# A one-core decoder trunk whose turned blocks land as whole block rows, and whose next reader puts them in order

## The chip, the cores and the metric

The kernel runs on one core of a Trainium2 chip. The metric is the device time of one execution in microseconds. TensorE (PE in the rows) multiplies, VectorE (DVE) and ScalarE (ACT) work elementwise, GpSimd (POOL) does a few powers and transfers, SyncE (SP) issues nearly all transfers. Each engine works through its own list in order, and semaphores tie the lists together.

## The reference

One layer over 256 positions of width 2048. A normalised input is projected by one wide matrix; three branches of width 1024 read slices of the result: a gated linear recurrence (A), a sparse attention with compressed, selected and window keys (B), and a softmax attention with a cumulative forget bias (C). Each branch output is gated, projected to 2048, weighed and summed; two more 2048 x 2048 products follow.

```python
z = split_columns(rms_norm(h, ln_gain) @ w_in + b_in)
y_a = rglru_branch(z['lru_x'], ...) * silu(z['lru_gate'])
q_b = rms_norm(split_heads(z['nsa_q'], 8), nsa_q_gain)
k_s = rms_norm(split_heads(z['nsa_k_slc'], 2), nsa_k_gain)   # k_w and k_c alike
y_b = nsa_branch(q_b, k_c, v_c, k_s, v_s, k_w, v_w, g_b) * silu(z['nsa_gate'])
y_c = fox_branch(rms_norm(fox_q, fox_q_gain), rms_norm(fox_k, fox_k_gain), fox_v, log_f) * silu(z['fox_gate'])
merged = sum(sigmoid(merge)[i] * (y_i @ w_branch[i]) for i in range(3))
h = h + merged @ w_out
h = h + sigmoid(h @ w_ple_gate) * rms_norm(p @ w_ple, ple_gain)
```

A gain of a query and a gain of its keys multiply the same channel of one dot product.

## The kernel before

**Weights.** All weights stream once from memory as 384 blocks of 128 x up to 1024 numbers (`raw`, five buffers, L399). ScalarE rounds each block to a short format (`wh`) and VectorE takes the rest (`wl`, L416): one *cut*. Each product is three matmuls, `wh` by the high half, `wl` by the high half, `wh` by the low half of the other factor (L382). The three blocks at the start are cut in smaller pieces, so that the cut with number n on ScalarE, counted from 0, belongs to block n - 4. A block of 1024 columns of the wide projection is 12 matmuls of 512 columns; a compression block ("cmp", every fourth or so from block 26 on) is 8 short ones. There are four pairs of `wh` and `wl` (L413), so cut n can start only when TensorE has left block n - 8. The transfer of block n into `raw` is issued when cut n - 5 is done.

**Side work.** Between blocks run generators (norms, LRU steps, attention tasks). A planner with a clock of its own (`Clock`, `Side`, L156 to L320) takes steps from them while VectorE and ScalarE are less than `LIMITS` behind TensorE; it writes the order of every engine. Everything is recorded through one helper, so the profile puts all on L206 and rows are told apart by the names of tiles.

**Turning.** A block with positions on partitions is turned to channels on partitions by `cross` (L654): VectorE transposes 32 x 32 cells into `zt`, and four transfers on SyncE's queue, one for each group of 32 partitions, put the cells in their place, each cell row of 32 numbers (128 bytes) at its own address (L667). `landed` then lets the planner wait `LAND`, 7000 ns of its clock. The gate and `lru_x` chunks are turned by `turn_chunk` (L673) and read by `silu_cols` and `biased_cols`; queries and keys by `norm_rows` (L842); the softmaxes inside `nsa_task` (L879) and `fox_task` (L990); the merged rows and h by `split_turned` (L1069). There are 41 such groups of four transfers.

**Factors.** Queries are scaled by their gain over sqrt(128) (`gqn`, `gqf`), keys by theirs (`vcol("nk")`, `vcol("fk")`), each in the split.

**LRU.** `lru_task` (L710) has four instances; each puts a table load, eight sigmoids, two tanh, a table load, two exponentials, a square and a root on ScalarE.

Of the kernel before, what the change touches and what calls it, by code (L numbers as in the profile page):

```python
# [323 lines left out]
def block_kernel(ctx: ExitStack, tc: tile.TileContext, io):  # L324
# [265 lines left out]
    def vec_task():  # L590
        a = VEC["lru_gate"]
        V.tensor_scalar(vec[:, a:], vec[:, a:], 0.5, None, op0=OP.mult)
        nl = sml([P, 8], name="nl")
        V.tensor_scalar(nl, vec[:, VEC["lam"]:VEC["lam"] + 8], -1.0, None, op0=OP.mult)
        yield from softplus(spc, nl, 8)
        V.tensor_scalar(spn, spc, -8.0, None, op0=OP.mult)
        V.tensor_scalar(spc, spc, 8.0, None, op0=OP.mult)
        V.tensor_scalar(gqn, vcol("nq"), SCALE, None, op0=OP.mult)
        V.tensor_scalar(gqf, vcol("fq"), SCALE, None, op0=OP.mult)
        yield True  # L600
# [31 lines left out]
    def silu_cols(dst, k0, src, name):  # L632
        for c in range(2):
            hb = vcol(name, k0 + c)
            t = one([P, S], name="th")
            x = dst[:, k0 + c, :]
            A.activation(t, src[:, c * S:(c + 1) * S], AF.Tanh, bias=hb, scale=0.5)
            A.activation(x, src[:, c * S:(c + 1) * S], AF.Identity, bias=hb, scale=0.5)
            V.scalar_tensor_tensor(x, t, 1.0, x, op0=OP.add, op1=OP.mult)

    def biased_cols(dst, k0, src, name):
        for c in range(2):
            A.activation(dst[:, k0 + c, :], src[:, c * S:(c + 1) * S], AF.Identity, bias=vcol(name, k0 + c))

# [28 lines left out]
    def turn_chunk(read, out, into, dst, k0, name):  # L673

        yield from side.wait("rs")
        yield from side.room(k4=1)
        x = flat(dst[:, k0:k0 + 4, :])
        for t, z in enumerate(celled(x)):
            A.activation(z, cells(out[t]), AF.Copy, scale=rsr[:, t:t + 1])
        side.done.add(read)  # L680
        yield from cross(x, x)
        side.give(k4=1)
        yield from side.wait("vec")
        for q in range(0, 4, 2):
            into(dst, k0 + q, flat(dst[:, k0 + q:k0 + q + 2, :]), name)
            yield True

    def turn_cmp(read, out, into, dst, k0, name):

        yield from side.wait("rs")  # L690
        z = [two([P, 512], name="z") for _ in range(NT)]
        for t in range(NT):
            A.activation(z[t], out[t], AF.Copy, scale=rsr[:, t:t + 1])
            yield True
        side.done.add(read)
        yield from side.settle()
        yield from side.wait("vec")
        for q in range(2):
            b, = yield from side.take()
            for c in range(2):  # L700
                for t in range(NT):
                    T.transpose(banks[b][:, c * S + t * P:c * S + (t + 1) * P],
                                z[t][:, (2 * q + c) * P:(2 * q + c + 1) * P], ident)
            yield True
            into(dst, k0 + 2 * q, banks[b], name)
            side.back(b)
            yield True
# [89 lines left out]
    def cmp_end():  # L797
# [39 lines left out]
        yield from side.wait("kk")  # L837
        split(st["kh"][:, :, 256:256 + NCMP], st["kl"][:, :, 256:256 + NCMP], src, vcol("nk"))
        side.back(b)
        yield True  # L840

    def norm_rows(z, n, dst):  # L842
# [10 lines left out]
        yield from side.powers()  # L853
        yield from side.room(k4=1)
# [24 lines left out]
    def nsa_task(g, pr, t):  # L879
# [3 lines left out]
        n = t + 1  # L883
        yield from side.room(k1=3, k4=2)
        qh, ql = one([P, 2, P], R32, name="qh"), one([P, 2, P], R32, name="ql")
        split(qh, ql, qn[:, heads[0]:heads[0] + 2, t, :], gqn)
        yield from side.settle()
# [3 lines left out]

        p, pz = mid([P, 4, 4 * n, 32], name="prob"), mid([P, 4, 4 * n, 32], name="pz")
        ps = p.rearrange("p b n j -> p (b n j)").rearrange("p (a w k) -> p a w k", a=2, w=2)
# [41 lines left out]
        yield from cross(pt, pt, p)  # L935
        side.give(k4=1)
        yield from side.room(k4=2)
        pth, ptl = mid([P, 2 * n, 2, P], R32, name="pth"), mid([P, 2 * n, 2, P], R32, name="ptl")
        split(*(x.rearrange("p i a q -> p (i a q)") for x in (pth, ptl)), pt)
        side.give(k4=1)  # L940
        yield True
# [18 lines left out]
        T.matmul(out, vc3[:, g, :], pct.rearrange("p a q -> p (a q)"), start=False, stop=True)  # L960
        side.give(k1=2, k4=2)
        yield True
        A.activation(qn[:, heads[0]:heads[0] + 2, t, :], out.rearrange("p (a q) -> p a q", a=2), AF.Copy)
        side.back(b)
# [25 lines left out]
    def fox_task(h):  # L990
# [40 lines left out]
        pth, ptl = two([P, 3 * P], R32, name="fpth"), two([P, 3 * P], R32, name="fptl")  # L1031
        split(pth, ptl, pt)
        side.give(k2=1)
# [5 lines left out]
        yield True  # L1039
        A.activation(fq[:, h].rearrange("p t d -> p (t d)"), banks[b][:, :S], AF.Copy)  # L1040
        side.back(b)
        yield True


    def y_split(name, src, names, gate=None):
        yield from side.wait(*names)
# [4 lines left out]
        for i in range(0, 8, 2):  # L1051
            s = src[:, i:i + 2, :]
            if gate is not None:
                V.tensor_tensor(s, s, gate[:, i:i + 2, :], op=OP.mult)
            split(yh[:, i:i + 2, :], yl[:, i:i + 2, :], s)
            side.done.add(f"{name}{i // 2}")
            yield True

    def start(name):
        if name == "ysplit0":  # L1060
            side.urge(name, y_split(name, st["yl"], [f"lru{q}" for q in range(4)] + ["gl0", "gl1"], st["gl"]))
        elif name == "ysplit1":
# [5 lines left out]

    def split_turned(name, dst, j, x, src, scale=None):  # L1069

        hi, lo = dst[j // 2]
        yield from cross(flat(x), src)
        for k in range(0, 4, 2):
            to = slice(4 * (j % 2) + k, 4 * (j % 2) + k + 2)
            split(hi[:, to, :], lo[:, to, :], x[:, k:k + 2, :], scale)
            yield True


    def rows_task(h, out, bias):
# [27 lines left out]
        else:  # L1107
            key = "fq" if what == "fox_q" else "fk"
            if c == 0:
                st[key] = big([P, 8, NT, P], name=key)  # L1110
            side.urge(f"{key}{c}", norm_rows(z, 512, st[key][:, 4 * c:4 * c + 4].rearrange("p h t d -> p (h t d)")))

# [45 lines left out]
    def proj_chunk(h, out):  # L1158
# [12 lines left out]
        if b == 2:  # L1171
            if j == 0:
                st["mt"] = [(big([P, 8, S], R32, name="mth"), big([P, 8, S], R32, name="mtl")) for _ in range(2)]
            side.urge(f"mt{j}", split_turned(f"mt{j}", st["mt"], j, x, flat(x), 0.5))

    def out_chunk(h, out):
# [158 lines left out]

LAND = 7000.0
LIMITS = 4500.0, 4000.0
# [77 lines left out]
```

## Time and profile before

| what | value |
|---|---|
| time, median of 3 runs | 1074.43 us (1072.45 to 1078.02) |
| the profiled execution: its time, its span | 1075.37 us, 1073.6 us |
| TensorE busy | 1061.1 us, 99% of the span |
| VectorE, ScalarE busy | 770.2 us, 619.1 us |
| transfers of SyncE's queue | 192320 packets, 220.75 MB |
| packets under 512 bytes, all queues | 140984 of 197255 |

Busy time of TensorE is modelled and overlaps from matmul to matmul, so a row of busy time shows where it waited, and the distance between starts shows how much was lost.

### The profile page before, as it was taken

The numbers are of one execution on the slowest core, as the hardware profiler recorded it, in microseconds if no ns is written. First come the engines' busy times: TensorE is split into PE (matmuls) and PEld (weight loads), VectorE is DVE, ScalarE is ACT, GpSimd is POOL, SyncE is SP. The second block draws the span as 40 slices with busy tenths as digits, with TensorE's granted clock in tenths as the row PEclk, the third lists the DMA queues.
The fourth block names the chain that finished last, engine by engine and source line by source line (L and its number), as shares of the span: only waits on it lengthen the run. The fifth ranks groups of instructions, "written<-read, shape, count | busy, mean of one in ns | idle before, by whom it ended". The sixth has DMA issues, their size and how long they took to land.

```text
span 1073.6 us, 14079 instructions
## 1 busy us (share of the span) xinstructions
PE 1061.1 (99%) x4943; PEld 884.0 (82%) x4943; DVE 770.2 (72%) x1127; ACT 619.1 (58%) x905; POOL 51.9 (5%) x77
## 2 busy tenths in 40 slices
PE   9999999999999999999999999999999999999997
PEld 7888788788888888887888888888888888888886
DVE  7787689688678787878787776555766566666664
ACT  7568975895676556545654565465555444444442
POOL 0000001011000000011101000000000100000000
PEclk9999999999999999999999999999999999999999
DMA  9768677768777577577787676777677887788762
GB/s 339 220 207 255 209 202 216 278 219 236 210 228 203 162 212 228 144 219 231 226 241 215 207 235 176 226 211 212 198 220 240 257 254 213 232 244 260 278 209 78
DMA packets 197255, 237.54 MB, mean 221 GB/s; under 512 B 140984, under 2 KB 142144, under 8 KB 197184
## 3 DMA queue, kind: packets, MB, share of 16 engines
q1 hardware_dynamic: 192320, 220.75, 66.6%
q0 software_dynamic: 4720, 15.76, 5.6%
q8 instruction: 38, 0.62, 0.2%
q14 instruction: 33, 0.27, 0.1%
q10 hardware_dynamic: 144, 0.14, 0.0%
HBM read 215.62 MB, written 4.20 MB: 205 GB/s over the span
## 4 chain that ended last, share of the span: by engine, by line
PE 88%; ACT 4%; DVE 4%; issue 2%; DMA 1%; SPq 1%; ACTq 0%; DVEq 0%
PE main L206 84%; PE bank L206 4%; ACT wh L206 2%; DVE wl L206 2%; DMA raw<-in_w 1%; SPq L206 1%; ACT k_lru L206 1%; ACT L206 0%; ACT k_gl L206 0%; ACT k_th L206 0%; DVE k_uc L206 0%; DVE k_yl L206 0%; DVE k_qn L206 0%; DVE k_z L206 0%; DVE k_fq L206 0%
## 5 line engine op out<-in xcount | busy, mean ns | idle before, releaser
L206 DVE TENSOR_TENSOR wl<-raw,wh 128x1024 fp32r<-128x1024 f32 (+2 forms) x388 | 459.4, 1198 | 244.0 <-ACT wh L206 243.1
L206 ACT ACTIVATE wh<-raw 128x1024 fp32r<-128x1024 f32 (+2 forms) x388 | 398.8, 1039 | 319.9 <-PE main L206 258.5
L206 PE MATMUL main<-wl,k_hnh 128*128 128x512 f32 (+2 forms) x1026 | 394.9, 386 | 4.1 <-DVE wl L206 3.7
L206 PE MATMUL main<-wh,k_hnh 128*128 128x512 f32 (+2 forms) x1026 | 396.0, 387 | 2.2 <-ACT wh L206 2.1
L206 PE MATMUL main<-wh,k_hnl 128*128 128x512 f32 (+1 forms) x1024 | 393.4, 384 | 0.0
L206 PEld LDWEIGHTS main<-wl,k_hnh 128*128 128x128 f32 x1026 | 193.6, 189 | 43.3 <-DVE wl L206 7.1
L206 PEld LDWEIGHTS main<-wh,k_hnh 128*128 128x128 f32 x1026 | 193.4, 189 | 40.6 <-ACT wh L206 4.1
L206 PEld LDWEIGHTS main<-wh,k_hnl 128*128 128x128 f32 x1024 | 193.0, 189 | 37.9
L206 PE MATMUL main<-wh,k_yh 128*128 128x512 f32 x192 | 75.2, 392 | 0.0
L206 PE MATMUL main<-wh,k_yl 128*128 128x512 f32 x192 | 74.8, 389 | 0.0
L206 PE MATMUL main<-wl,k_yh 128*128 128x512 f32 x192 | 74.8, 389 | 0.0
L206 PE MATMUL main<-wh,k_mth 128*128 128x512 f32 x128 | 49.8, 389 | 0.0
L206 PE MATMUL main<-wl,k_mth 128*128 128x512 f32 x128 | 49.8, 389 | 0.0
L206 PE MATMUL main<-wh,k_mtl 128*128 128x512 f32 x128 | 49.8, 389 | 0.0
L206 PE MATMUL main<-wh,k_hth 128*128 128x512 f32 x128 | 49.8, 389 | 0.0
L206 PE MATMUL main<-wl,k_hth 128*128 128x512 f32 x128 | 49.8, 389 | 0.0
L206 PE MATMUL main<-wh,k_htl 128*128 128x512 f32 x128 | 49.8, 389 | 0.0
L206 PEld LDWEIGHTS main<-wh,k_yl 128*128 128x128 f32 x192 | 36.0, 188 | 7.6
L206 PEld LDWEIGHTS main<-wh,k_yh 128*128 128x128 f32 x192 | 36.1, 188 | 7.1
L206 PEld LDWEIGHTS main<-wl,k_yh 128*128 128x128 f32 x192 | 36.1, 188 | 7.0
L206 ACT ACTIVATE k_mg<-k_mg 128x512 f32<-128x512 f32 x24 | 15.2, 632 | 24.3 <-DVE k_mg L206 24.0
L206 PEld LDWEIGHTS main<-wh,k_mth 128*128 128x128 f32 x128 | 24.0, 188 | 5.0
(247 smaller groups left out, 965.8 us busy)
## 6 DMA issues: line engine op xcount, KB each, us to landing
raw<-in_w SPq DMA_DIRECT2D x369, 512.0 KB, 4.7
bias<-in_b_in POOLq DMA_DIRECT2D x21, 256.0 KB, 5.7
raw<-in_w SPq DMA_DIRECT2D x8, 408.0 KB, 4.4
k_pz<-k_prob SPq DMA_DIRECT2D x16, 128.0 KB, 4.1
e_dram<-k_e POOLq DMA_DIRECT2D x4, 512.0 KB, 3.6
k_merged<-k_zt SPq DMA_DIRECT2D x16, 128.0 KB, 3.3
k_xc<-in_x POOLq DMA_DIRECT2D x4, 512.0 KB, 5.4
k_hx<-k_zt SPq DMA_DIRECT2D x16, 128.0 KB, 3.3
```

What stands on the lines that cost most here:

```text
L206: r = call(out, *args, **kw)
```

## The change

`cross` no longer puts each 128-byte cell row in its place. Each of the four transfers writes to each partition its four whole block rows, of 1024 bytes at a full block, and the reader takes the cells in order by its access pattern (`moved`, `moved_heads`; `blocks` is the same view of a block already in order). `turn_chunk` now lands in a separate `zt` of 1024 columns. The gain of the keys is folded into `gqn` and `gqf`, the queries are split without a scale, and the key splits are made per 128 columns, since a moved view has one dimension more. The factor 0.5 of the merged rows moves to `out_chunk`. The four sparse tasks with t = 0 take their probability tiles from the pool `k2` of half-size tiles instead of `k4`. The norms of `fq` and `fk` wait for the sparse tasks and for `ysplit13`. `LAND` is 5500.

```diff
-        V.tensor_scalar(gqn, vcol("nq"), SCALE, None, op0=OP.mult)
+        V.scalar_tensor_tensor(gqn, vcol("nq"), SCALE, vcol("nk"), op0=OP.mult, op1=OP.mult)
...
+    def blocks(x):
+        return x.rearrange("p (n a j) -> p n a j", a=4, j=32)
+    def moved(x):
+        return x.rearrange("p (a n j) -> p n a j", a=4, j=32)
+    def moved_heads(x, h0, h1):
+        c = h0 // 4
+        z = x[:, 4 * c:4 * c + 4].rearrange("p h t d -> p (h t d)").rearrange("p (a h t j) -> p h t a j", a=4, h=4, j=32)
+        return z[:, h0 - 4 * c:h1 - 4 * c]
...
-        to = dst.rearrange("p (n a j) -> p n a j", a=4, j=32)
+        to = dst.rearrange("p (a m) -> p a m", a=4)
         for a in range(4):
-            Q.dma_start(to[:, :, a, :], zt[32 * a:32 * a + 32].rearrange("p b n j -> p (b n) j"))
+            Q.dma_start(to[:, a, :], zt[32 * a:32 * a + 32].rearrange("p b n j -> p b (n j)"))
...
-        x = flat(dst[:, k0:k0 + 4, :])
+        x = mid([P, 4 * S], name="zt")
...
-        yield from cross(x, x)
-        side.give(k4=1)
+        yield from cross(x, x, flat(dst[:, k0:k0 + 4, :]).rearrange("p (b n j) -> p b n j", b=4, j=32))
         yield from side.wait("vec")
         for q in range(0, 4, 2):
-            into(dst, k0 + q, flat(dst[:, k0 + q:k0 + q + 2, :]), name)
+            into(dst, k0 + q, moved(x)[:, 2 * q:2 * q + 4], name)
             yield True
+        side.give(k4=1)
...
-                split(st["kh"][:, :, c:c + P], st["kl"][:, :, c:c + P], zn[:, 2 * sw:2 * sw + 2, t, :], vcol("nk"))
+                splits(*((*(st[x][:, g, c:c + P].rearrange("p (a j) -> p a j", a=4) for x in ("kh", "kl")),
+                          moved_heads(zn, 2 * sw + g, 2 * sw + g + 1)[:, 0, t], gqn) for g in range(2)))
...
-        splits(*((hi, lo, x[:, h].rearrange("p t d -> p (t d)"), gain)
-                 for hi, lo, x, gain in ((qh, ql, fq, gqf), (kh, kl, fk, vcol("fk")))))
+        qt, kt = (moved_heads(x, h, h + 1)[:, 0] for x in (fq, fk))
+        splits((blocks(qh), blocks(ql), qt, None),
+               *((blocks(kh)[:, t], blocks(kl)[:, t], kt[:, t], gqf) for t in range(NT)))
...
-            V.tensor_tensor(st["h"][j // 2][:, t, 512 * (j % 2):512 * (j % 2) + 512], out[t], st["xc"][:, t, :], op=OP.add)
+            V.scalar_tensor_tensor(st["h"][j // 2][:, t, 512 * (j % 2):512 * (j % 2) + 512], out[t], 0.5,
+                                   st["xc"][:, t, :], op0=OP.mult, op1=OP.add)
...
-LAND = 7000.0
+LAND = 5500.0
```

**Place 1: SyncE's list around the turned keys** (`zn`, cut 76 and after; `raw` are weight blocks). Before:

```order
L206 DMA raw_1709<-in_w 128x1024
L206 DMA raw_1723<-in_w 128x1024
L206 DMA k_zn_1524<-k_zt_1629 128x8x32 x4
L206 DMA raw_1762<-in_w 128x1024
L206 DMA raw_1793<-in_w 128x1024
```

And now:

```order
L206 DMA raw_1688<-in_w 128x1024
L206 DMA raw_1716<-in_w 128x1024
L206 DMA k_zn_1535<-k_zt_1637 128x1x256 x4
L206 DMA raw_1739<-in_w 128x1024
L206 DMA raw_1773<-in_w 128x1024
```

The four transfers stand one weight block earlier, and each goes from 8 x 32 numbers on every partition to one run of 256.

**Place 2: ScalarE's list at the first LRU tasks** (`k_lru` are gates and their tanh and exponentials, `wh_1011` is cut 42 before and `wh_979` is cut 40 now). Before:

```order
L206 ACTIVATE k_lru_999<-bank_88,vec 64x256
L206 ACTIVATE wh_1011<-raw_935 128x1024
L206 ACTIVATE wh_1029<-raw_953 128x1024
L206 ACTIVATE k_lru_1000<-k_lru_998,spc 128x256 x2
L206 ACT_TABLE_LOAD
L206 ACTIVATE k_lru_998<-k_lru_998,spn 128x256 x2
L206 ACTIVATE wh_1056<-raw_984 128x1024
```

And now:

```order
L206 ACTIVATE k_lru_956<-bank_88,vec 64x256
L206 ACTIVATE k_lru_957<-k_lru_955,spc 128x256 x2
L206 ACT_TABLE_LOAD
L206 ACTIVATE k_lru_955<-k_lru_955,spn 128x256 x2
L206 ACTIVATE wh_979<-raw_899 128x1024
L206 ACTIVATE wh_998<-raw_915 128x1024
```

The table load and eight sigmoids that stand ahead of these rows in both lists were ahead of cut 42 and are ahead of cut 40; the tanh, the second table load and the exponentials, which had two cuts between them and the sigmoids, now follow at once.

**Place 3: ScalarE's list after the turned keys** (`kk` are the keys' splits; `wh_1834` is cut 77 before, `wh_1844` is cut 76 now). Before:

```order
L206 ACTIVATE wh_1834<-raw_1762 128x1024
L206 ACTIVATE kk<-k_zn_1524,vec 128x2x128 x2
L206 ACTIVATE wh_1857<-raw_1793 128x1024
L206 ACTIVATE wh_1871<-raw_1811 128x1024
L206 ACTIVATE kk<-k_zn_1524,vec 128x2x128 x2
L206 ACTIVATE wh_1893<-raw_1832 128x1024
L206 ACTIVATE wh_1913<-raw_1855 128x1024
```

And now:

```order
L206 ACTIVATE wh_1810<-raw_1716 128x1024
L206 ACTIVATE kk<-k_zn_1535,gqn 128x128 x8
L206 ACTIVATE wh_1844<-raw_1739 128x1024
L206 ACTIVATE wh_1862<-raw_1773 128x1024
L206 ACT_TABLE_LOAD
L206 ACTIVATE k_lru_1882<-bank_88,vec 64x256
```

The keys' splits were two and two with two cuts between them; now eight stand ahead of cut 76, and an LRU task's table load and sigmoids, which stood ahead of cut 84, stand ahead of cut 78 (its tanh, table load and exponentials ahead of cut 80).


## Rows read from the trace of the kernel before

**Rows 1.** The page: engines over the whole span (busy us, share, instructions).

```profile
PE 1061.1 (99%) x4943; PEld 884.0 (82%) x4943; DVE 770.2 (72%) x1127; ACT 619.1 (58%) x905; POOL 51.9 (5%) x77
```

**Rows 2.** Busy time by stretches: PE, PEld, DVE, ACT, POOL, clock, DMA share, GB/s.

```profile
150.00:175.00 25.00, 22.97 (x166) 21.27 (x165) 23.93 (x39) 16.73 (x25) 3.29 (x4) 1.00 0.56 172
191.00:194.00 3.00, 3.00 (x8) 2.31 (x7) 3.00 (x5) 2.54 (x4) 0.54 (x1) 0.50 0.97 385
450.00:475.00 25.00, 25.00 (x123) 20.97 (x122) 19.41 (x22) 11.93 (x16) 3.14 (x2) 1.00 0.63 181
```

**Rows 3.** The chain that ended last: start us, us, what.

```profile
673.70 394.51 PE main L206 x1740
```

**Rows 4.** Timeline of PE: start us, us, what, idle time before and its releaser.

```profile
103.10 0.39 PE L206 MATMUL main<-wh,k_hnh 128*128 128x512 f32 x1
...
122.09 0.39 PE L206 MATMUL main<-wh,k_hnl 128*128 128x512 f32 x1
123.22 0.50 PE L206 MATMUL main<-wh,k_hnh 128*128 128x512 f32 x1 [0.74 <-ACT wh L206]
124.48 0.50 PE L206 MATMUL main<-wl,k_hnh 128*128 128x512 f32 x1 [0.76 <-DVE wl L206]
...
190.41 0.50 PE L206 MATMUL main<-wl,k_hnh 128*128 128x512 f32 x1 [0.76 <-DVE wl L206]
...
198.27 0.39 PE L206 MATMUL main<-wh,k_hnh 128*128 128x512 f32 x1
```

**Rows 5.** Timeline of SP's issues around two turned groups.

```profile
134.92 5.06 SPq L206 DMA_DIRECT2D k_gl<-k_zt  x4
140.08 1.88 SPq L206 DMA_DIRECT2D raw<-in_w  x3
...
176.62 6.52 SPq L206 DMA_DIRECT2D k_zn<-k_zt  x4
183.23 0.72 SPq L206 DMA_DIRECT2D raw<-in_w  x1
```

**Rows 6.** SP's issues by tile: ns min/median/max of one.

```profile
L206 SPq DMA_DIRECT2D k_xT<-in_xT x9: 327/423/442, 1.7 to 18.5; - x9
L206 SPq DMA_DIRECT2D k_gl<-k_zt x8: 615/782/4563, 102.2 to 139.3; - x8
```

**Rows 7.** SP's queue from 134 to 143 us, then from 143 to 150: packets, MB, DMA share.

```profile
q1 hardware_dynamic: 4508, 1.82, 88.6%
...
q1 hardware_dynamic: 722, 2.26, 91.4%
```

**Rows 8.** Timeline of ACT from 92 to 190 us: cuts and LRU work.

```profile
92.37 1.06 ACT L206 ACTIVATE wh<-raw 128x1024 fp32r<-128x1024 f32 x1 [1.76 <-DMA raw<-in_w]
...
100.32 1.28 ACT L206 ACT_TABLE_LOAD   x1
101.61 3.88 ACT L206 ACTIVATE k_lru<-bank,vec 64x256 f32<-64x256 f32 x8
...
109.64 0.91 ACT L206 ACTIVATE k_lru<-k_lru,spn 128x256 f32<-128x256 f32 x2
...
178.75 1.06 ACT L206 ACTIVATE wh<-raw 128x1024 fp32r<-128x1024 f32 x1
...
188.04 1.06 ACT L206 ACTIVATE wh<-raw 128x1024 fp32r<-128x1024 f32 x1 [4.26 <-DMA raw<-in_w]
```

**Rows 9.** Timeline of DVE near 85 us: LRU convolutions and cuts.

```profile
83.72 1.52 DVE L206 SCALAR_TENSOR_TENSOR k_uc<-k_u,vec,k_uc 128x255 f32<-128x255 f32 x3
85.16 2.35 DVE L206 TENSOR_TENSOR wl<-raw,wh 128x1024 fp32r<-128x1024 f32 x2
```

**Rows 10.** Splits by shape: count, busy us, mean ns of one, idle before.

```profile
L206 ACT ACTIVATE kk<-k_zn,vec 128x256 fp32r<-128x256 f32 x4 | 1.8, 494 | 0.0
L206 ACT ACTIVATE kk<-bank,vec 128x30 fp32r<-128x30 f32 x1 | 0.3, 287 | 0.4 <-PE bank L206 0.4
```

**Rows 11.** Transfers that readers waited for: who, us in total, times, longest.

```profile
ACT k_mth L206 <- DMA k_merged<-k_zt: 0.7, 1, 0.7
```

More of the change, by code (lines that the diff above doesn't have):

```diff
@@ L635, in silu_cols @@
             t = one([P, S], name="th")
-            x = dst[:, k0 + c, :]
-            A.activation(t, src[:, c * S:(c + 1) * S], AF.Tanh, bias=hb, scale=0.5)
-            A.activation(x, src[:, c * S:(c + 1) * S], AF.Identity, bias=hb, scale=0.5)
+            x, z = dst[:, k0 + c, :], src[:, 2 * c:2 * c + 2]
+            A.activation(blocks(t), z, AF.Tanh, bias=hb, scale=0.5)
+            A.activation(blocks(x), z, AF.Identity, bias=hb, scale=0.5)
             V.scalar_tensor_tensor(x, t, 1.0, x, op0=OP.add, op1=OP.mult)
@@ L642, in biased_cols @@
         for c in range(2):
-            A.activation(dst[:, k0 + c, :], src[:, c * S:(c + 1) * S], AF.Identity, bias=vcol(name, k0 + c))
+            A.activation(blocks(dst[:, k0 + c, :]), src[:, 2 * c:2 * c + 2], AF.Identity, bias=vcol(name, k0 + c))
+    def blocks(x):
[6 more added lines that the diff above has]
+        return z[:, h0 - 4 * c:h1 - 4 * c]
     def cells(x):
@@ L704, in turn_cmp @@
             yield True
-            into(dst, k0 + 2 * q, banks[b], name)
+            into(dst, k0 + 2 * q, blocks(banks[b]), name)
             side.back(b)
@@ L837, in cmp_end, with norm_rows @@
         yield from side.wait("kk")
-        split(st["kh"][:, :, 256:256 + NCMP], st["kl"][:, :, 256:256 + NCMP], src, vcol("nk"))
+        split(st["kh"][:, :, 256:256 + NCMP], st["kl"][:, :, 256:256 + NCMP], src, gqn)
         side.back(b)
         yield True
-    def norm_rows(z, n, dst):
+    def norm_rows(z, n, dst, after=()):
         m = n // P
@@ L853, in norm_rows @@
         yield from side.powers()
+        yield from side.wait(*after)
         yield from side.room(k4=1)
@@ L883, in nsa_task @@
         n = t + 1
-        yield from side.room(k1=3, k4=2)
+        tile_of, size = (mid, "k4") if t else (two, "k2")
+        yield from side.room(k1=3, **{size: 2})
         qh, ql = one([P, 2, P], R32, name="qh"), one([P, 2, P], R32, name="ql")
-        split(qh, ql, qn[:, heads[0]:heads[0] + 2, t, :], gqn)
+        qt = moved_heads(qn, heads[0], heads[0] + 2)[:, :, t]
+        split(*(x.rearrange("p h (a j) -> p h a j", a=4) for x in (qh, ql)), qt)
         yield from side.settle()
@@ L935, in nsa_task @@
         yield from cross(pt, pt, p)
[L936 to L940, printed above, removed]
+        side.give(**{size: 1})
+        yield from side.room(**{size: 2})
+        pth, ptl = (tile_of([P, 2 * n, 2, P], R32, name="pt") for _ in range(2))
+        split(*(blocks(x.rearrange("p i a q -> p (i a q)")) for x in (pth, ptl)), moved(pt))
+        side.give(**{size: 1})
         yield True
@@ L960, in nsa_task @@
         T.matmul(out, vc3[:, g, :], pct.rearrange("p a q -> p (a q)"), start=False, stop=True)
-        side.give(k1=2, k4=2)
+        side.give(k1=2, **{size: 2})
         yield True
-        A.activation(qn[:, heads[0]:heads[0] + 2, t, :], out.rearrange("p (a q) -> p a q", a=2), AF.Copy)
+        A.activation(qt, blocks(out), AF.Copy)
         side.back(b)
@@ L1031, in fox_task @@
         pth, ptl = two([P, 3 * P], R32, name="fpth"), two([P, 3 * P], R32, name="fptl")
-        split(pth, ptl, pt)
+        split(blocks(pth), blocks(ptl), moved(pt))
         side.give(k2=1)
@@ L1039, in fox_task, with y_split @@
         yield True
-        A.activation(fq[:, h].rearrange("p t d -> p (t d)"), banks[b][:, :S], AF.Copy)
+        A.activation(qt, blocks(banks[b][:, :S]), AF.Copy)
         side.back(b)
         yield True
-    def y_split(name, src, names, gate=None):
+    def y_split(name, src, names, gate, heads=True):
         yield from side.wait(*names)
@@ L1051, in y_split @@
         for i in range(0, 8, 2):
[L1052 to L1055, printed above, removed]
+            if heads:
+                s = moved(flat(src[:, i // 4 * 4:i // 4 * 4 + 4, :]))[:, 2 * (i % 4):2 * (i % 4) + 4]
+                y, z, g = (blocks(flat(x[:, i:i + 2, :])) for x in (yh, yl, gate))
+            else:
+                s, y, z, g = (x[:, i:i + 2, :] for x in (src, yh, yl, gate))
+            V.tensor_tensor(s, s, g, op=OP.mult)
+            split(y, z, s)
             side.done.add(f"{name}{i // 2}")
@@ L1060, in start @@
         if name == "ysplit0":
-            side.urge(name, y_split(name, st["yl"], [f"lru{q}" for q in range(4)] + ["gl0", "gl1"], st["gl"]))
+            side.urge(name, y_split(name, st["yl"], [f"lru{q}" for q in range(4)] + ["gl0", "gl1"], st["gl"], False))
         elif name == "ysplit1":
@@ L1074, in split_turned @@
             to = slice(4 * (j % 2) + k, 4 * (j % 2) + k + 2)
-            split(hi[:, to, :], lo[:, to, :], x[:, k:k + 2, :], scale)
+            split(*(blocks(flat(y[:, to, :])) for y in (hi, lo)), moved(flat(x))[:, 2 * k:2 * k + 4])
             yield True
@@ L1110, in rows_task @@
                 st[key] = big([P, 8, NT, P], name=key)
-            side.urge(f"{key}{c}", norm_rows(z, 512, st[key][:, 4 * c:4 * c + 4].rearrange("p h t d -> p (h t d)")))
+            side.urge(f"{key}{c}", norm_rows(z, 512, st[key][:, 4 * c:4 * c + 4].rearrange("p h t d -> p (h t d)"),
+                                              NSA if key == "fq" else ["ysplit13"]))
     def vs_task(z, c):
@@ L1173, in proj_chunk @@
                 st["mt"] = [(big([P, 8, S], R32, name="mth"), big([P, 8, S], R32, name="mtl")) for _ in range(2)]
-            side.urge(f"mt{j}", split_turned(f"mt{j}", st["mt"], j, x, flat(x), 0.5))
+            side.urge(f"mt{j}", split_turned(f"mt{j}", st["mt"], j, x, flat(x)))
     def out_chunk(h, out):
```

6 lines of the change are left out of this document (3 added, 3 removed).

## The prediction

> **What bounds the kernel now.** I read the page's busy shares first. The reader is to see TensorE at 1061.1 of 1073.6 us and the other engines far below [rows 1]. The chain that ended last then shows 1740 matmuls in 394.51 us without a break, 226.7 ns each [rows 3]. I take this as the cadence; a block of 12 such matmuls is 2.72 us. Wherever two starts stand further apart, the difference is lost time. Adding up such differences over all matmuls by stretches of 25 us, I find about 19 us of loss in the span: 5.3 before the first blocks run, 5.8 behind the last matmul, and about 8 between 100 and 200 us; the rest is small and scattered. Head and tail are not touched by the change. So the change can give back about 10 us at most, 1%; it can cost more.
>
> Where are the 8 us? The timeline of TensorE shows a pair of waits at 123.22 and 124.48: starts are 1.13 and 1.26 us apart, so 0.90 and 1.03 are lost, first waiting for `wh` from ScalarE and then for `wl` from VectorE [rows 4]. The same pair ends at 190.41 [rows 4], and from 191 to 194 us the clock stands at 0.50, so that 3.0 us of matmuls make 1.5 us of progress [rows 2]; over 3.4 us at half clock this is 1.7 us. Between 150 and 175 us TensorE is busy for 22.97 of 25 us [rows 2] in six or seven short waits on `wl`; by the distances of starts they lose 3.7 us, by the idle time alone 2.0.
>
> Why are the cuts late? I read SyncE's issues next. A turned group of four held SyncE for 5.06 us from 134.92, and the weight blocks behind it went out only at 140.08; another held it for 6.52 us from 176.62, and the next block went out at 183.23 [rows 5]. ScalarE then sat 4.26 us with nothing but that block to wait for, until cut 77 at 188.04 [rows 8]. This is the stall at 190. The one at 123 has another cause: an LRU table load and its sigmoids (1.28 + 3.88 us, as at 100.32 [rows 8]) and two more splits stood ahead of one cut.
>
> **What the new transfers remove.** A turned transfer takes 615 ns to issue at least, and up to 4563 in these groups; a transfer of the activations with long rows takes 327 to 442 [rows 6]. After the change each of the four writes 1024 bytes in a run, not 32 numbers at a time. I put a group at 1.3 to 2.5 us by the two medians and minima (4 x 0.33 to 4 x 0.62), against 5.06 and 6.52. The blocks behind them then go out 3 to 5 us sooner, about as much as they were late: the pair at 190 goes with the half clock, 1.9 + 1.7 = 3.6 us, and most of the waits from 150 to 175, for which I take 3.2 between 2.0 and 3.7; it is the least certain of the three, since VectorE is busy 23.93 of 25 us there [rows 2], in part because it catches up. The pair at 123 goes too, 1.9, since the burst ahead of it is moved (below). Gone: 3.6 + 3.2 + 1.9 = 8.7 us.
>
> The same stretch shows what the transfers carry: from 134 to 143 us, 1.82 MB in 4508 packets took 88.6% of 9 us, 4.4 us of all 16 engines per MB; from 143 to 150, 2.26 MB in 722 packets took 2.8 per MB [rows 7]. Short packets are dear here. A section of the Trainium skill speaks against this: "Why small descriptors are slow (HBM only)", in DMA: Bandwidth & Descriptors, says that transfers within SBUF don't suffer the penalty of small descriptors. By that rule the transfers would get no shorter and the blocks no earlier, which is the last rival below; the trace disagrees, with 4.4 against 2.8 us per MB and with the issue times of [rows 6].
>
> **What the change of order adds.** With readers due 1500 ns earlier and other pools, the planner places side work in other gaps, and the cuts stand behind it. I followed each list from cut to cut.
>
> (a) VectorE: one LRU convolution more, four instructions at 0.47 to 0.51 us (three for 1.52 [rows 9]), 1.9 us, stands ahead of cut 28. Cuts here are used hardly half a microsecond after they end (the pair of cuts that begins at 85.16 ends about 86.4 or 87.5 [rows 9], its blocks follow at once), so by the smaller slack about 1.9 - 0.9 = 1.0 us is lost.
>
> (b) ScalarE: all of an LRU task, 1.28 + 3.88 + 0.9 + 1.28 + 0.91 = 8.25 us [rows 8], now stands ahead of cut 40; before, two cuts lay inside it. Cut 38 begins at 92.37 [rows 8]; with its own 1.06, 0.8 of side work and cut 39 the burst starts at 95.2, ends at 103.4, `wh` is ready at 104.5 and `wl` (about 1.2 for a cut [rows 9]) at 105.7. Block 36, which needs them, is due at 103.10 [rows 4]. TensorE waits 1.4 for the one and 1.0 more for the other: 2.4 us.
>
> (c) ScalarE: the next task's table load and sigmoids stand ahead of cut 44, 5.7 us with what lies beside them, where the ring of four cuts covers about two blocks, 5.4 us: 0.5 us with the wait for `wl`.
>
> (d) ScalarE from cut 76: eight key splits, then an LRU task's load and sigmoids (5.16), then tanh, load and exponentials with small copies (3.6). A key split of 256 columns takes 494 ns, one of 30 columns 287 [rows 10]; one of 128 columns isn't in the trace. Between these ends I take 415 ns, nearer to the longer since a view with one more dimension may cost something; eight are 3.3 us. From the end of cut 75 at 179.8 [rows 8] this is 3.3 + 5.16 + 3.6 + five cuts at 1.0 = 17.1, so that `wh` of cut 80 is ready at 196.9 and `wl` at 198.1. Block 76 started at 198.27 [rows 4]; without the 3.6 us of loss ahead of it it is due at 194.65. Lost: 3.5 us. Much of the gain at 190 is so given back eight microseconds later.
>
> New losses: 1.0 + 2.4 + 0.5 + 3.5 = 7.4 us. They are uncertain by half at least: the planner's own clock sees no stall in any of them, so they rest on my adding.
>
> **Edits that I cost at nothing.** Twenty-four splits of 128 columns replace twelve of 256 on each of ScalarE and VectorE: by the prices above 12 x (2 x 0.29 - 0.49) = 1.0 to 12 x 0.49 = 5.9 us more in the whole run on ScalarE. Sixteen of them lie in the last softmaxes, where TensorE is busy for 25.00 of 25 us, ScalarE for 11.93 and VectorE for 19.41 [rows 2]; matmuls hide them. If that cover were gone they would cost 0.2 to 0.5 us for each task. Folding the gains is two instructions in the head and no longer chain. The 0.5 of the merged rows moves into an addition that was there. Reading through a moved view could cost or save a little on each of some 60 instructions; they lie in the same stage. Smaller tiles for four tasks let these start earlier; norms that wait for the sparse tasks do the opposite. I take 0 for all of it, and -1 to +3 as its bounds.
>
> **Sum.** 1075.37 - 8.7 + 7.4 = 1074.1 us for the profiled execution. This lay 0.94 above the median of the runs shown, so in their terms 1073.2 us. Its own range is 1069 to 1078: half of (b) and (d) either way.
>
> **Rivals.**
> *The bursts are hidden.* If blocks arrive 3 to 5 us sooner, ScalarE may be further ahead of TensorE at cuts 40 and 76 than I reckon; the ring of cuts limits this to two or three blocks, 5 to 8 us, which speaks against it for (b) and (d), but a 25 us stretch at full speed would speak for it. Then only the gain is left: 1075.37 - 8.7 - 0.94 = 1065.7 us. Between this and the forecast lies the case in which one of (b) and (d) is hidden, 1068 to 1070.
> *Readers come before their data (slower).* The planner now places a reader 5500 ns behind its transfers, not 7000. If a group, from its issue to its last landing, takes longer than that, the reader waits at the head of ScalarE's list, with the next cut queued behind it, and TensorE behind this. With 7000 readers waited 0.7 us at the longest [rows 11], so the old lead was hardly too short; the issue alone was 5.06 and 6.52 us [rows 5]. It decides from about 5.5 us plus ScalarE's lead on. In the tight stage up to 290 us there are nine groups; at 1.5 us each that is 13.5, of which half is covered by the ring: +6.7, 1080.0 us with the other terms as they are, and with the half clock back 1081.7.
> *The change doesn't shorten the transfers.* SyncE stays at 615 ns and more for each; then the stalls from 150 to 194 stay (6.8 us) and the bursts come on top: 1073.2 + 6.8 = 1080.0. [Rows 6] and [rows 7] speak against it.
>
> **Numbers.** Forecast 0.54, hidden bursts 0.29, early readers 0.11, no shorter transfers 0.06. About 0.5% (5.4 us) is what a measurement of this kernel can tell from no change: faster is below 1069.1, slower above 1079.8. Faster: nearly all of the second case and the lower edge of the first, 0.31. Slower: most of the last two and the upper edge of the first, 0.17. The same: 0.52. The range that leaves out about 2 in 10 is 1066 to 1080.5.
>
> **What would show it.** Right: SyncE's groups at 1.3 to 2.5 us and no `raw` late behind them near 135 and 178; no gap near 190 and no half clock there; gaps of TensorE near 103 and between 194 and 198, released by ScalarE and then VectorE. Wrong: no gap at 103 or 196 (the bursts were hidden); ScalarE waiting on turned transfers for over a microsecond at a time; groups still at 5 us; or, beyond all cases, TensorE below 25 of 25 us after 300 us, where I have put every edit at nothing.

## The result, and the profile after

| kernel | median | ratio to before, 95% interval |
|---|---|---|
| before, beside it | 1074.24 us (4 runs) | 1 |
| changed | 1082.27 us (1081.59 to 1083.54, 4 runs) | 1.0073 [1.0056, 1.0090] |

The changed kernel is slower by 8 us, 0.7%. The forecast was 1073.2, with a range that ended at 1080.5, and "the same" as the likeliest outcome. Its profiled execution took 1082.16 us, with a span of 1080.4 us, 6.8 more than before.

The first row answers [rows 1]; the second is the page's row on SyncE's queue (packets, MB, share of 16 engines).

```profile
PE 1063.2 (98%) x4943; PEld 883.3 (82%) x4943; DVE 770.9 (71%) x1139; ACT 616.9 (57%) x917; POOL 52.4 (5%) x77
...
q1 hardware_dynamic: 81216, 220.75, 63.3%
```

No engine has noticeably more work: VectorE has 0.7 us more, ScalarE 2.2 less. The 192320 packets on SyncE's queue have become 81216, for the same 220.75 MB. (Both traces have 156 turned transfers, 39 groups of four, not the 41 that the section on the kernel before gives.) So the time is in waits. SyncE's groups (start us, us, what) answer [rows 5]:

```profile
135.13 3.19 SPq L206 DMA_DIRECT2D k_zt<-k_gl  x4
...
172.49 3.07 SPq L206 DMA_DIRECT2D k_zn<-k_zt  x4
```

They hold SyncE for 3.1 to 3.2 us where they held it for 5.06 and 6.52. ScalarE's cuts wait for weight blocks for 3.5 us in the whole run, where they waited for 25.6. And the stretches (columns as in [rows 2]) show where TensorE waits:

```profile
100.00:125.00 25.00, 23.34 (x116) 18.84 (x115) 14.02 (x14) 24.72 (x37) 0.54 (x1) 1.00 0.66 224
150.00:175.00 25.00, 24.88 (x187) 23.96 (x186) 24.51 (x41) 15.38 (x27) 2.89 (x3) 1.00 0.62 189
175.00:200.00 25.00, 22.19 (x126) 18.46 (x125) 18.40 (x35) 21.64 (x38) 0.54 (x1) 1.00 0.71 246
200.00:225.00 25.00, 23.10 (x102) 18.69 (x101) 17.13 (x26) 20.73 (x30) 0.54 (x1) 0.93 0.63 211
```

From 150 to 175 us TensorE is busy for 24.88 us, where it was 22.97 [rows 2]: nearly all of those waits are gone. The next two stretches have 22.19 and 23.10. The timeline of TensorE names the places; they answer [rows 4]:

```profile
104.54 0.50 PE L206 MATMUL main<-wh,k_hnh 128*128 128x512 f32 x1 [0.51 <-ACT wh L206]
105.80 0.50 PE L206 MATMUL main<-wl,k_hnh 128*128 128x512 f32 x1 [0.76 <-DVE wl L206]
...
191.10 0.50 PE L206 MATMUL main<-wh,k_hnh 128*128 128x512 f32 x1 [0.45 <-ACT wh L206]
192.36 0.50 PE L206 MATMUL main<-wl,k_hnh 128*128 128x512 f32 x1 [0.76 <-DVE wl L206]
...
196.42 0.50 PE L206 MATMUL main<-wh,k_hnh 128*128 128x512 f32 x1 [0.37 <-ACT wh L206]
197.68 0.50 PE L206 MATMUL main<-wl,k_hnh 128*128 128x512 f32 x1 [0.75 <-DVE wl L206]
...
208.95 0.50 PE L206 MATMUL main<-wh,k_hnh 128*128 128x512 f32 x1 [1.14 <-ACT wh L206]
210.22 0.79 PE L206 MATMUL main<-wl,k_hnh 128*128 128x512 f32 x1 [0.76 <-DVE wl L206]
...
404.31 0.50 PE L206 MATMUL main<-wl,k_hnh 128*128 128x512 f32 x1 [1.09 <-DVE wl L206]
```

Each pair is one late cut: first `wh`, then `wl`. ScalarE's list ahead of the first pair is the run of which the prediction spoke:

```profile
95.22 1.28 ACT L206 ACT_TABLE_LOAD   x1
96.52 3.87 ACT L206 ACTIVATE k_lru<-bank,vec 64x256 f32<-64x256 f32 x8
100.41 0.91 ACT L206 ACTIVATE k_lru<-k_lru,spc 128x256 f32<-128x256 f32 x2
101.34 1.28 ACT L206 ACT_TABLE_LOAD   x1
102.63 0.91 ACT L206 ACTIVATE k_lru<-k_lru,spn 128x256 f32<-128x256 f32 x2
103.45 2.94 ACT L206 ACTIVATE wh<-raw 128x1024 fp32r<-128x1024 f32 x3
```

And ahead of the pair at 209, where cut 84 is the first of the four in the last row:

```profile
202.44 0.22 ACT L206 ACTIVATE sp_spl<-sp_spl 128x16 f32<-128x16 f32 x1 [2.30 <-DVE sp_spl L206]
202.66 1.28 ACT L206 ACT_TABLE_LOAD   x1
203.96 3.86 ACT L206 ACTIVATE k_lru<-bank,vec 64x256 f32<-64x256 f32 x8
207.84 3.90 ACT L206 ACTIVATE wh<-raw 128x1024 fp32r<-128x1024 f32 x4
```

Here ScalarE first stands 2.30 us, at a small copy that waits for VectorE, then runs 5.1 us of LRU work, and only then cuts. During the second wait of this pair TensorE's granted clock falls to 0.50, the lower of its two levels (1.2 of 2.4 GHz), and stays there from 210.1 to 213.5 us, as it did before from 190.9 to 194.3.

Adding up the distances of starts beyond the cadence, as the prediction did, gives 25.5 us of loss, 6.5 more than the 19.0 of before:

| stretch (us) | before | after |
|---|---|---|
| 75 to 100 | 0 | 1.1 |
| 100 to 125 | 2.0 | 2.5 |
| 150 to 175 | 3.7 | 0.7 |
| 175 to 200 | 4.0 | 4.2 |
| 200 to 225 | 0 | 4.0 |
| 275 to 300 | 0 | 0.8 |
| 375 to 425 | 0.3 | 2.7 |

The rest of the span differs by little. What is to be explained is not a resource that runs out but why cuts are late in other places.

### The profile page after: what moved, and what is told of

The parts are those of the page before. It is cut to its first block, busy times and chain, and to the rows that moved or that the text cites. A ratio compares the mean times of both kernels' runs of the same rounds, so it can differ in the third digit from the quotient of the medians.

```text
span 1080.4 us, 14108 instructions
## 1 busy us (share of the span) xinstructions
PE 1063.2 (98%) x4943; PEld 883.3 (82%) x4943; DVE 770.9 (71%) x1139; ACT 616.9 (57%) x917; POOL 52.4 (5%) x77
## 3 DMA queue, kind: packets, MB, share of 16 engines
q1 hardware_dynamic: 81216, 220.75, 63.3%
## 4 chain that ended last, share of the span: by engine, by line
PE 86%; ACT 5%; DVE 5%; DMA 2%; issue 2%; SPq 0%; DVEq 0%; ACTq 0%
PE main L206 82%; PE bank L206 4%; DVE wl L206 2%; ACT wh L206 2%; DMA raw<-in_w 2%; ACT k_lru L206 1%; DMA k_zn<-k_zt 1%; DVE k_uc L206 1%; ACT k_pz L206 0%; ACT L206 0%; SPq L206 0%; ACT k_u L206 0%; ACT kk L206 0%; DVE k_pz L206 0%; DVE k_zn L206 0%
## 5 line engine op out<-in xcount | busy, mean ns | idle before, releaser
L206 PEld LDWEIGHTS main<-wl,k_hth 128*128 128x128 f32 x128 | 24.0, 188 | 5.0
```

The costliest lines, as they stand in the source:

```text
L206: r = call(out, *args, **kw)
```

## The experiments

My theory after the result: the new transfers do save time, and the new order of side work costs more than they save. Rivals: readers 1.5 us nearer behind their transfers cost the time; or the moved views and the 128-column splits do; or the transfers are worth nothing. All kernels ran beside the kernel before; the ratios are to it. Three groups of runs had their own runs of before (medians of 1073.53, 1074.58 and 1074.59 us: e1 to e4, e5 to e8, e9 to e11), so a difference between two kernels is given by their medians and by their ratios where these part.

**The planner's clock.** Why does an edit of transfers move an LRU task? `Clock.add` charges an entry only after earlier ones whose range of addresses, from the lowest to the highest, overlaps its own, and for a transfer after their end plus 2000 ns. The four old transfers interleave, so each was charged behind the one before; the four new ones lie side by side and are charged without those 2000 ns between them. With its readers' data ready sooner by its clock, the planner lets more steps follow each other without a cut between. This much is read from the code; e1 and e5 test it.

**e1: new transfers, the charge of the old ones, LAND 7000.**

```diff
-            Q.dma_start(to[:, a, :], zt[32 * a:32 * a + 32].rearrange("p b n j -> p b (n j)"))
+            nc.sync.dma_start(to[:, a, :], zt[32 * a:32 * a + 32].rearrange("p b n j -> p b (n j)"))
+            at = dst.rearrange("p (n a j) -> p n a j", a=4, j=32)[:, :, a, :]
+            clock.add("d", at.shape[0] * at.shape[1] * at.shape[2] * 4 / 331.0, at, [], 2000.0)
...
-LAND = 5500.0
+LAND = 7000.0
```

> The changed kernel, its transfers as they are, but the planner's clock is charged as if the four turned transfers still interleaved (each after the one before, plus 2000 ns), and LAND is 7000 again. ScalarE's list then has its long runs of side work before cuts 42, 48, 52 and 84 as the kernel before has them, none of 8 us before cut 40, none before cut 78. Theory (the changed order costs the time, the transfers save some): no waits of TensorE at 104 and from 184 to 213 us, SyncE's groups at about 2.4 us, the pair of waits near 122 stays; 1068 to 1072 us. Rival (reading moved views, the 128-column splits, or the readers themselves cost it): 1079 to 1083 us, like the changed kernel.

1078.84 us, 1.0046 [1.0031, 1.0060]. By the medians this is 3 us faster than the changed kernel, but the two intervals just overlap, and it lies 7 us above the range of the theory, at the edge of the rival's. So the time alone decides nothing here; the trace does. The waits at 104 and from 184 to 198 are gone. One that I had not foreseen is new:

```profile
316.84 0.80 PE L206 MATMUL main<-wh,k_yh 128*128 128x512 f32 x1 [3.62 <-ACT k_yh L206]
```

This is no cut but the fourth of the four splits of branch A's product, which the planner had put late; the clock falls to half at the end of this wait. Waits near 200 us (2.3 and the half clock) stay too.

**e2: old transfers in the order of e1.** Against e1, `cross` writes cells of 128 bytes in place and `moved` reads blocks in order; the planner is charged by the transfers themselves, and the lists of ScalarE and VectorE stand as in e1 but for the shapes.

```diff
-        to = dst.rearrange("p (a m) -> p a m", a=4)
+        to = dst.rearrange("p (n a j) -> p n a j", a=4, j=32)
...
-            Q.dma_start(to[:, a, :], zt[32 * a:32 * a + 32].rearrange("p b n j -> p b (n j)"))
+            Q.dma_start(to[:, :, a, :], zt[32 * a:32 * a + 32].rearrange("p b n j -> p (b n) j"))
```

> As e1 with almost the same order on every engine, but the turned transfers write cells of 128 bytes in place again and readers read blocks in order. The other edits (joined factors, 128-column splits, smaller tiles, later norms) are in. Theory: SyncE's groups take 4 to 6.5 us again, weight blocks behind them go out late near 135 and 178, and the time is 3 to 7 us above e1: 1073 to 1078 us. Rival (transfers are worth nothing): equal to e1 within 1 us. If the other edits cost the time: 1080 us or more here too.

1084.32 us, 1.0112 [1.0093, 1.0132]: 5.5 us above e1 by the medians, 7 by the ratios, within what the theory asks for the difference or at its edge, while both lie higher than expected. The third case of the expectation (1080 us or more here too, if other edits cost the time) has come true as well. In SyncE's timeline the group that e1 issues in 2.54 us takes 7.05 here:

```profile
175.27 7.05 SPq L206 DMA_DIRECT2D k_zn<-k_zt  x4
```

ScalarE waits for weight blocks 27.3 us in all (e1: 9.7). So the transfers are worth something, but something besides them makes e2 10 us slower than the kernel before, with the same transfers. The losses of e2 differ from before's by the same late split near 320 us with its half clock (5.8 us) and by smaller waits at 208, 390, 451. Which of the other edits puts the split late, no run separates; e8 and e9 show that the loss isn't tied to them, since with all of them in, another order is faster than the kernel before.

**e3: the changed kernel, its LRU tasks paused.**

```diff
                 A.activation(inp[own[s], c, :], g[other[s]], AF.Sigmoid, bias=vcol("bx", ct)[other[s]])
+            yield from side.settle()
         side.back(*bs)
-        yield True
```

> The changed kernel, with one edit in lru_task: after each four sigmoids the generator waits until the planner's TensorE clock has passed what was issued, so that cuts come between. The 8.4 us before cut 40 fall to 3.2, likewise before cuts 44, 78 and 84; a run of 5.1 us remains before cut 60 and one of 5.7 before cut 75. Theory (runs of LRU work ahead of cuts cost the time): of the losses at 104 to 116 us (2.3), 184 to 198 (3.9) and 207 to 213 (2.7 and 1.7 of half clock) about 7 to 10 go; 1072 to 1076 us. Rival (the readers of turned blocks or the moved views): 1080 to 1083 us.

1074.33 us, 1.0011 [1.0001, 1.0020]: 8 us regained by the medians, 6.7 by the ratios, by an edit that takes no work away. The run before cut 40 is now parted by cuts (`wh`):

```profile
96.71 1.93 ACT L206 ACTIVATE k_lru<-bank,vec 64x256 f32<-64x256 f32 x4
98.66 1.06 ACT L206 ACTIVATE wh<-raw 128x1024 fp32r<-128x1024 f32 x1
...
101.33 1.91 ACT L206 ACTIVATE k_lru<-bank,vec 64x256 f32<-64x256 f32 x4
103.27 2.96 ACT L206 ACTIVATE wh<-raw 128x1024 fp32r<-128x1024 f32 x3
```

TensorE is busy for 25.00 of 25 us from 100 to 125 and from 200 to 225 in this run, and its clock never falls between head and tail. Moved views, splits and LAND are those of the changed kernel; by themselves they can't have made these 7 to 8 us. The pauses move all side work behind them, so they show that the order cost this time, not which of its runs cost how much.

**e4: old transfers in the changed kernel's order.** `cross` and `moved` as in e2, but the planner charged as for the new transfers, so that the long runs stand where the changed kernel has them.

```diff
+            nc.sync.dma_start(to[:, :, a, :], zt[32 * a:32 * a + 32].rearrange("p b n j -> p (b n) j"))
+            at = dst.rearrange("p (a m) -> p a m", a=4)[:, a, :]
+            clock.add("d", at.shape[0] * at.shape[1] * 4 / 331.0, at, [], 2000.0)
```

> The changed kernel with cells of 128 bytes landing in place, while the planner's clock is charged as in the changed kernel, so that ScalarE's long runs stand before cuts 40, 44, 78, 84, 88 and 110 as there. Theory: both losses, late weight blocks and long runs: 1084 to 1090 us. Rival (the new transfers are worth nothing): 1081 to 1083 us. Rival (the transfers and not the order made the changed kernel slower): 1074 to 1078 us.

1086.09 us, 1.0113 [1.0097, 1.0129], as the theory expected; 4 us above the changed kernel. Up to 300 us its waits stand within 2 us of the changed kernel's places, and TensorE is busy for 22.41 us between 100 and 125 where the changed kernel has 23.34. From 330 to 405 us its lists differ from the changed kernel's, and the waits at 388 and 404 aren't there, so the 4 us aren't the price of the transfers alone.

**e5 and e6: LAND alone.** The changed kernel with `LAND = 7000.0`, and with `LAND = 4500.0`.

> The changed kernel with LAND at 7000 as before, nothing else. ScalarE's list then has 8.5 us of side work before cut 76 and 8.4 before cut 80 (changed kernel: 3.4 and 3.6, with 5.1 before cut 78), and 5.1 before cuts 40, 44 and 59. Theory (runs of side work ahead of cuts set the time, the lead of the readers does not): better near 104, far worse near 186, with waits of TensorE of about 5 us there and half clock behind them; 1084 to 1090 us, slower than the changed kernel. Rival (readers that come 1.5 us earlier cost the time): 1074 to 1078 us.

> The changed kernel with LAND at 4500, nothing else: readers stand still nearer behind their transfers. The order has 5.1 us before cut 39, 5.7 before 44, 5.6 before 80 and 5.1 before 86, and never 8; VectorE's longest run before a cut falls from 6.6 to 5.6 us. Theory: fewer and shorter waits than in the changed kernel, 1074 to 1079 us. Rival (a short lead costs the time): ScalarE waits for turned transfers by more than the 5 us in total of the changed kernel, 1084 us or more.

1092.12 us, 1.0171 [1.0157, 1.0185], and 1078.22 us, 1.0045 [1.0031, 1.0058]. The longer lead is 10 us slower (2 us above the range that I gave), the shorter one 3 to 4 us faster, with intervals that just overlap: the opposite of what readers that come too early would do. At 4500 a reader does wait 4.2 us once for the turned keys, and it is still the faster. At 7000 the run that counts is this, with the key splits, load and sigmoids ahead of cut 76 (first of four):

```profile
187.48 1.26 ACT L206 ACTIVATE kk<-k_zn,gqn 128x128 fp32r<-128x128 f32 x4
188.76 1.28 ACT L206 ACT_TABLE_LOAD   x1
190.06 3.86 ACT L206 ACTIVATE k_lru<-bank,vec 64x256 f32<-64x256 f32 x8
193.93 1.28 ACT L206 ACTIVATE kk<-k_zn,gqn 128x128 fp32r<-128x128 f32 x4
195.11 3.88 ACT L206 ACTIVATE wh<-raw 128x1024 fp32r<-128x1024 f32 x4
```

and TensorE:

```profile
196.21 0.79 PE L206 MATMUL main<-wh,k_hnh 128*128 128x512 f32 x1 [6.04 <-ACT wh L206]
```

e5 and e1 have the same transfers, the same LAND and the same work; only what the planner's clock charges differs. That is 13.3 us.

**e7: e3 with LAND at 7000.**

> The paused LRU tasks of e3, with LAND at 7000. With the runs gone in both, this against e3 is the price of the readers' lead alone. No run over 5 us is left in ScalarE's list, one of 6.6 before cut 28 in VectorE's. Theory: the same as e3 within 2 us, 1072 to 1076 us. Rival: readers that come early cost something, so 3 us or more below e3, under 1071.5 us.

1075.69 us, 1.0018 [1.0008, 1.0029]. Where the runs are gone, 1.5 us of lead more make 0.7 us by the ratios, whose intervals overlap, and not in the rival's direction; e5, which differs only in the pauses, is 16 us slower.

**e8: e3 with `LIMITS = 3500.0, 3000.0`.**

> The paused LRU tasks of e3, with LIMITS at 3500 and 3000 ns in place of 4500 and 4000, so that the planner stops side work sooner. VectorE's 6.6 us before cut 28 become 2.9 and 2.9; ScalarE's longest runs are 5.1 before cuts 46 and 55. Theory: the waits near 81 and 181 go too, and the new transfers' saving remains; 1067 to 1071 us, below both kernels. Rival (there is a cost of the edits that no order takes away): 1073 us or more.

1072.06 us, 0.9976 [0.9967, 0.9985]: faster than both kernels, a microsecond short of the range. The wait near 81 us is gone, the one near 181 is not (1.0 us lost), and a new one of 1.5 us stands at 54. The late split is still there:

```profile
311.24 0.50 PE L206 MATMUL main<-wh,k_yh 128*128 128x512 f32 x1 [2.28 <-ACT k_yh L206]
```

**e9: e8, the last two splits of branch A in one step.**

```diff
             side.done.add(f"{name}{i // 2}")
-            yield True
+            if heads or i != 4:
+                yield True
```

> e8 with one more edit: the last two of the four steps in which branch A's product is split stand together, so that the planner can't put 8 us between them. In e8 (and in e1, e3 and e7) TensorE waited 2 to 4 us near 310 us for the fourth of these splits, and in three of the four the clock went to half behind it. Theory: this wait and the half clock go, 4 us; 1067 to 1070 us. Rival: the wait moves to another reader; 1071 to 1073 us as e8.

1070.68 us, 0.9952 [0.9934, 0.9969]; just above the range, and the fastest of all. The wait for `k_yh` is gone, 0.51 us for a `wl` stands near its place, and the clock doesn't fall. The profiled execution, 1068.56 us, shows this (the whole span, then two of the stretches):

```profile
PE 1055.3 (99%) x4943; PEld 881.4 (83%) x4943; DVE 771.1 (72%) x1139; ACT 617.4 (58%) x918; POOL 51.7 (5%) x77
```

```profile
175.00:200.00 25.00, 24.33 (x127) 20.51 (x126) 22.73 (x42) 14.62 (x27) 0.54 (x1) 1.00 0.90 308
200.00:225.00 25.00, 25.00 (x123) 20.95 (x122) 21.03 (x31) 20.76 (x29) 2.79 (x3) 1.00 0.70 224
```

**e10: old transfers in the order of e9** (the edit of e4 on e9).

> e9 with cells of 128 bytes landing in place and blocks read in order, while the planner's clock is charged as in e9, so that every engine's list stands as in e9. The price of the transfers in an order without long runs. Theory: SyncE's groups at 4 to 6.5 us make weight blocks late as in the kernel before, with waits between 150 and 195 us; 3 to 6 us above e9, so 1071 to 1075 us. Rival (transfers only matter where runs of side work have used up the slack): within 1 us of e9.

1072.97 us, 0.9981 [0.9968, 0.9994]: 2.3 us above e9 by the medians and 3.1 by the ratios, less than expected or just within it, and at the limit of what these runs tell apart (the intervals just touch). The group of the keys takes SyncE 6.06 us against 3.01 in e9, and TensorE is busy for 23.34 us from 175 to 200 against 24.33. So the new transfers saved 5.5 to 7, about 4 (with lists that part from 330 us on) and 2 to 3 us in three orders, and least in the one without long runs. Of the 0.5% by which e9 is faster than the kernel before, the order gives about 0.2% by this run and the transfers the rest.

**e11: the changed kernel with full-size tiles for the tasks with t = 0.**

```diff
-        tile_of, size = (mid, "k4") if t else (two, "k2")
+        tile_of, size = (mid, "k4")
```

> The changed kernel with the four sparse tasks of t = 0 in the pool of full-size tiles again. ScalarE's list is the same up to cut 110; VectorE's has 13.4 us of side work before cut 180 where the changed kernel has under 4.6. Theory (runs ahead of cuts cost the time): a wait of TensorE of about 5 us near 485 us, perhaps with half clock behind it; 1086 to 1090 us, so the smaller tiles are a gain. Rival (the smaller tiles start tasks earlier and so crowd the lists): 1078 to 1081 us.

1090.56 us, 1.0139 [1.0123, 1.0155]: 7 to 8 us above the changed kernel. The two waits at 388 and 404 us are gone, and for these come

```profile
499.22 0.79 PE L206 MATMUL main<-wh,k_hnh 128*128 128x512 f32 x1 [4.79 <-ACT wh L206]
502.12 0.80 PE L206 MATMUL main<-wl,k_hnh 128*128 128x512 f32 x1 [2.11 <-DVE wl L206]
```

behind a run of norms, a transposition and splits on VectorE. The smaller tiles are a gain in this order. The waits at 388 and 404 can't be put down to them: e4 has the smaller tiles too, and not these waits.

The norms' waits for the sparse tasks and for `ysplit13` weren't run: without them the program that is built is the changed kernel's, instruction for instruction, so they change nothing.

## Why the prediction was wrong

**Right: what the transfers remove.** Of the 8.7 us, the waits from 150 to 175 fell by 3.0 (3.2 forecast), and the pair at 123 and the pair at 190, with the late weight block and the half clock, are gone: 8.6 us. The sign "no gap near 190" is not to be seen all the same, since one of the late cuts of (d) stands at 191. The groups were mis-sized: 2.5 to 3.2 us, not 1.3 to 2.5, since the shortest issue only fell from 615 to 555 ns, and not to that of the activations [rows 6]:

```profile
L206 SPq DMA_DIRECT2D k_zt<-k_gl x8: 555/605/1264, 116.9 to 137.7; - x8
```

What went is the long ones, up to 4563 ns. It was enough. By the Trainium skill (DMA: Bandwidth & Descriptors, "Why small descriptors are slow (HBM only)"), transfers within SBUF don't suffer the penalty of small descriptors. These runs disagree: e2 and e1, with the same lists on ScalarE and VectorE, differ by 5.5 to 7 us and by 111,000 packets.

**(a) to (d): right in size, (d) in part by luck.** Run, cut and wait of (b) were put at 95.2, 104.5 and 105.7 us and stand at 95.22, 104.54 and 105.80. The loss is 1.7 and not 2.4, since (a) had already moved the block. Against 1.0, 2.4, 0.5 and 3.5 us stand 1.1, 1.7, 0.6 and 3.9: 7.3 in sum, 7.4 forecast. (d) came as three late cuts (185, 191 and 196 us), not one, and in another way than it was added up. Cut 75 ends at 178.6, not 179.8, the eight splits take 2.45 us, not 3.3, and ahead of them ScalarE waits for the turned keys, for which the sum had nothing:

```profile
177.51 1.06 ACT L206 ACTIVATE wh<-raw 128x1024 fp32r<-128x1024 f32 x1 [1.30 <-DMA raw<-in_w]
180.43 2.45 ACT L206 ACTIVATE kk<-k_zn,gqn 128x128 fp32r<-128x128 f32 x8 [1.86 <-DMA k_zn<-k_zt]
```

Of the 3.9 us up to 1.9 can be this wait; no run takes it out alone. The 128-column splits, put at 415 ns, take 389 on ScalarE and 348 on VectorE, one beside the other:

```profile
L206 ACT ACTIVATE kk<-k_zn,gqn 128x128 fp32r<-128x128 f32 x8 | 2.5, 389 | 1.9 <-DMA k_zn<-k_zt 1.9
L206 DVE SCALAR_TENSOR_TENSOR kk<-k_zn,gqn,kk 128x128 fp32r<-128x128 f32 x8 | 2.3, 348 | 0.0
```

In a row they start 307 ns apart (eight in 2.45 us), so even this estimate was high.

**The step that failed: "New losses: 1.0 + 2.4 + 0.5 + 3.5 = 7.4 us".** The list wasn't complete. It stops in (d) at cut 80, and the next loss comes at cut 84: 4.0 us, of which 2.3 are the pair at 209 and 1.7 the half clock. The run ahead of this cut is 6.0 us long in both kernels and begins right behind cut 83 in both, at 199.45 and 199.52 us. Before, its end and cuts 84 and 85 were these:

```profile
200.31 1.28 ACT L206 ACT_TABLE_LOAD   x1
201.60 3.87 ACT L206 ACTIVATE k_lru<-bank,vec 64x256 f32<-64x256 f32 x8
205.50 2.01 ACT L206 ACTIVATE wh<-raw 128x1024 fp32r<-128x1024 f32 x2
```

Cut 84 began at 205.50, in time for block 80 at 208.35. In the changed kernel the small copy `sp_spl`, which stood behind cut 87, stands inside the run; ScalarE waits 2.30 us for it, cut 84 begins at 207.84, and block 80 would have been due at 207.66. The wait alone doesn't do it either. In e9 ScalarE waits longer for the same copy, but a cut stands right behind it, and TensorE is busy without a break from 183 to 225 us:

```profile
199.28 0.22 ACT L206 ACTIVATE sp_spl<-sp_spl 128x16 f32<-128x16 f32 x1 [3.92 <-DVE sp_spl L206]
199.40 1.04 ACT L206 ACTIVATE wh<-raw 128x1024 fp32r<-128x1024 f32 x1
```

So a run that had been hidden and a wait that can be hidden made the loss together. This rests on three traces side by side; no run takes the wait alone out of the changed kernel. The sum treated the clock as a loss that goes with its stall; it returned with the next one.

**"Matmuls hide them" failed too.** I put the later stage at nothing, with -1 to +3 us as bounds, since TensorE was busy for 25.00 of 25 us [rows 2]. That row shows 450 to 475 us alone; the last softmaxes run from 505 us on, and were as full. The splits cost little there: TensorE waits for one of them at 513 and at 585 us, 0.34 us lost each time, 0.7 in sum.

```profile
513.47 0.84 PE L206 MATMUL bank<-k_fx,k_fx 128*128 128x128 f32 x5 [0.23 <-DVE k_fx L206]
```

But ahead of them the tasks stand in another order, and waits at 290, 388, 404 and 480 us lose 0.5, 0.9, 1.3 and 1.0, where before had one of 0.7: 3.0 us. Together this is 3.7 us, beyond the bounds. Why these waits fall on just these cuts stays open.

Gone 8.6, new 7.3 + 4.0 + 3.0 + 0.7 = 15.0: a balance of +6.4 of the 6.8 us of span; the rest are small waits that I have not placed. (The "about 8" us of loss between 100 and 200 us in the kernel before are 9.7 by the table above; no term of the prediction's sum rests on that figure.)

**The slower rival was the wrong one.** I gave 0.11 to readers that come before their data. The sign that I named for it came, since they wait 1.9, 1.8 and 1.3 us in the changed kernel, the first of them in (d). But e6 and e7 show that the lead has little price of its own, and e5, in which no reader waits for the turned keys, is 10 us slower. LAND works through the order: 4500, 5500 and 7000 give 1078, 1082 and 1092 us, and with the LRU tasks paused 5500 and 7000 differ by a microsecond. The prediction named LAND and the pools as what moves the order; the charge for the transfers, which it didn't name, is worth at least as much (13.3 us between e1 and e5, against 10 between the changed kernel and e5). My chance for slower, 0.17, was too small for a forecast that rested on the difference of two sums of 8 us, when the sum of losses could only be incomplete in one direction: losses that were not looked for.

## What to carry to other kernels

Where a planner writes the order, an edit that changes what the planner is charged is a change of the whole order, and should be timed against a kernel in which only the charge is changed: here the charge alone was worth 13 us, the transfers 2 to 7. A late cut depends on how long the work ahead of it is and on the waits inside that work; follow every list past the last difference that looks large, and ask of each small step that has moved what it waits for. And where a large step of side work stands ahead of a short due one, a pause inside it took no work away and gave back 7 to 8 us; with tighter limits and one joined step the kernel with the new transfers is 0.5% faster than before.

## What the runs showed of the hardware

The four transfers of the turned keys, 1024 bytes to a partition each, held SyncE for 7.05 and 6.06 us when they went as rows of 128 bytes (e2, e10), and for 2.54 and 3.01 us as whole rows (e1, e9), with the same lists on ScalarE and VectorE.

A late cut cost its waits (1.7 us at 104 us in the changed kernel) and sometimes a half clock on top (2.3 and 1.7 at 209). In ten of the thirteen traces TensorE's clock fell to 0.5 between head and tail, each time during a wait or within 2 us behind one, and stayed there for 3.4 us (6.8 in one place of e1 and of e5, 10.2 in e11, where TensorE stood for part of this). A like wait didn't always do it: the pair at 190 in the kernel before lost 1.94 and the clock fell, while the pair at 123 of the same run (1.93), the wait at 312 in e3 (1.95) and a pair at 185 in e10 (2.08) left it at full speed. What decides between them these runs don't show.
